# Norms between GEMMs in a two-layer encoder: one hand-ordered piece on TensorE, VectorE and ACT at each of four seams

## The chip, the cores and the metric

The kernel runs on one core of a Trainium2 chip. The metric is the device time of one execution in microseconds (us); a figure for a kernel is the median of its runs. TensorE (PE in the profile; PEld is its weight load) does the matmuls, VectorE (DVE) the elementwise arithmetic, ScalarE (ACT) the activation functions and casts, GpSimd (POOL) some elementwise work and the DMAs that it issues, SyncE (SP) most other DMAs. The kernel is written in a tile framework: a scheduler orders the instructions of every engine by priority (the order in which they are written) and by its own estimate of time, and places the semaphores. Inside `tc.manual_schedule(engines=...)` the named engines issue the region's instructions in the order in which they are written; where instructions from outside fall among them stays the scheduler's.

## The reference

Two layers over x of 1024 positions by 1024 channels, float32. Cut to what matters here:

```python
def rmsnorm(x, g):
    xf = x.astype(jnp.float32)
    y = xf * lax.rsqrt(jnp.mean(xf * xf, axis=-1, keepdims=True) + EPS)
    return (y * g.astype(jnp.float32)).astype(x.dtype)

def conv_ffn(h, w_up, conv_w, conv_b, w_down):
    gate, val = jnp.split(h @ w_up, 2, axis=-1)
    gate = dwconv3(gate, conv_w, conv_b)
    return (jax.nn.silu(gate) * val) @ w_down

    for i in range(DEPTH):
        ...
        h = rmsnorm(x, norm1_g[i]) * (1.0 + sc1) + sh1
        if m == 0:
            y = attention_mixer(h, ...)      # ends in o @ w_o
        elif m == 1:
            y = hyena_mixer(h, ...)          # starts with h @ w_in, ends in zc @ w_out
        x = x + g1 * y
        h = rmsnorm(x, norm2_g[i]) * (1.0 + sc2) + sh2
        x = x + g2 * conv_ffn(h, ffn_w_up[i], ffn_conv_w[i], ffn_conv_b[i], ffn_w_down[i])
    return rmsnorm(x, final_g)
```

So a GEMM's result is scaled and added to x, x is normed over its channels, and the next GEMM takes the normed h. This happens between w_o and w_up (layer 0), w_down and w_in (layer 0 to layer 1), w_out and w_up (layer 1), and between w_down and the output (layer 1). These are the four seams, in this order.

## The kernel before

x lies with channels on partitions: eight tiles (k or dt_, 0 to 7) of 128 channels by 1024 positions. Positions are taken in two halves of 512 (`HS`, hf). Every GEMM runs in three matmuls per product: each operand is split into a high part in fp32r and a low part (the rest), and high by high, high by low and low by high are added up in PSUM. A weight tile of 128 by 1024 is loaded raw by SP, cast to its high part by ACT (L169, 128x1024) and subtracted to its low part by DVE (L162), or the low part is read from DRAM by a DMA that POOL issues (L173). `wt` is a set of two weight buffers used in turn; `wraw` two raw buffers.

**A seam.** `tail_begin` gives half of the PSUM tiles of the GEMM to four small tiles: two for results ("yt"), two for the norm ("nrm"); results then take turns in two halves of big tiles and two "yt" (`pst_tail`). For each half hf, and each output tile dt_ in it: the GEMM's matmuls for 128 channels by 512 positions (24 matmuls in the first seam, 6 in the second, 12 in the third and fourth), then `res` (L857): DVE adds the scaled result to x (`scalar_tensor_tensor`, STT, L858), ACT squares it (L861), DVE adds the square to the running sum `ssq` (L863), except for the last tile of the half, whose square is kept apart. Then `rstd_half` (L223): for each of four blocks of 128 positions TensorE sums `ssq` over the partitions by a matmul with ones (L226), and the last square likewise on top (L227); each of these fp32 matmuls is two instructions. ACT takes the root (L229), DVE the reciprocal (L230), and four transposes on TensorE (L232) spread it over the partitions of the "nrm" tile. `norm_half` (L243) then makes h for each of the eight tiles (`modnorm`): DVE scales x (L236), ACT adds the shift and rounds to h's high part (L238), DVE subtracts for the low part (L239). In the fourth seam DVE makes the output tile (L1705) and SP writes it out.

**The GEMMs behind the seams.** w_up: `ffn` (L947) loads a gate and a value weight tile and calls `gemm_h` (L276); for the first pair (`first=True`) half 0 of both stands before half 1, 96 matmuls in all; the second pair, 96 more, loads its gate weights into another pool. Then `differences` prepares sums of x and h on DVE and ACT for the following stage. w_in: `w_in_stream` (L1224) takes tiles 0, 1 and 2 of w_in together: half 0 of tiles 0 and 1, half 0 of tile 2, then half 1 likewise; tile 2's weights go into a pool (`fpool`) that is opened in the memory that the FFN of layer 0 has freed. The filter stage that runs beside it (`F.run`) also begins its loads there.

**What orders the work at the seams.** The scheduler alone, on all engines: it may put half 1's matmuls before half 0's, delay an add, or run a weight split between norm operations. In the third seam x is not in SBUF: `x[k]` and the first half of the w_out product, `y0`, are read from DRAM and added by DVE (L1673), with two buffers for `y0`.

Of the kernel before, what the change touches and what calls it, by code (L numbers as in the profile page):

```python
# [7 lines left out]
F32 = mybir.dt.float32  # L8
# [107 lines left out]
def tile_kernel(ctx: ExitStack, tc: tile.TileContext, t: dict):  # L116
# [106 lines left out]
    def rstd_half(hf, sq, pool, yt):  # L223
        for j in range(4):
            c0 = 512 * hf + j * P
            mm(yt[:, j:j + 1], lhsT=ssq[:, c0:c0 + P], rhs=ones[:, 0:1], start=True, stop=False)  # L226
            mm(yt[:, j:j + 1], lhsT=sq[:, j * P:(j + 1) * P], rhs=ones[:, 0:1], start=False, stop=True)  # L227
# [15 lines left out]
    def norm_half(hf, x, l, which, hd, pool, rs, bufs=4):  # L243
        for k in range(KT):
# [31 lines left out]
    def gemm_h(prs, hd, n=KT, first=False, start=True, stop=True):  # L276
        if first:
            order = [(hf, k, p_, i) for hf in range(2) for k in range(n) for p_ in prs for i in range(3)]
        else:
            order = [(hf, k, p_, i) for p_ in prs for k in range(n) for i in range(3) for hf in range(2)]  # L280
        for hf, k, ((wh, wl), pp), i in order:
            ks = slice(k * P, (k + 1) * P)
            mm(pp[:, HS[hf]], lhsT=(wh, wh, wl)[i][:, ks], rhs=hd[hf][i % 2][k],  # L283
               start=k == 0 and i == 0, stop=k == n - 1 and i == 2)

# [571 lines left out]
    def res(yp, x_t, g, cs, first, sq, last=False):  # L857
# [4 lines left out]
        if not first and not last:  # L862
            V.tensor_tensor(ssq[:, cs], ssq[:, cs], sq, op=ADD)  # L863
# [974 lines left out]
```

## Time and profile before

| | |
|---|---|
| median of 3 runs | 3000.87 us (2999.51 to 3001.46) |
| profiled execution | 2999.89 us |
| its span, first to last instruction | 2998.1 us |
| mean granted TensorE clock | 0.979 |
| PE busy | 2834.4 us, 95% |
| DVE busy | 2289.6 us, 76% |
| ACT busy | 1228.0 us, 41% |

How to read it: the page's first part gives each engine's busy time; its fourth part the chain of work that ended last, as shares of the span. In a line of the timeline stand the start in us from the span's start, the duration, the engine, the line of the kernel, the operation, output<-input by tile names, shape, and in brackets how long the engine had been idle before it and what ended that. In a line of the chain stand start, duration, engine, output and line. A waits line gives who waited for whom, the total in us, how often, and the longest. A windows line gives a stretch, its length, busy time and instruction count of each engine, the mean granted clock of TensorE (1.00 is full speed, 0.50 half), the DMA engines' share and GB/s. Tile names: wo_y, d_ps and wout_y are the results of w_o, w_down and w_out; g_ps and v_ps those of w_up; u_ps of w_in; xr, xd, xs are x in the three stages; fh_h, fh_l, gh_h, gh_l are h's high and low parts; tt is scaled x.

### The profile page before, as it was taken

Reading aid. Unit: us, or ns where it says so; the run is one execution under the profiler, and the core shown is the slowest. Engines: PE = TensorE matmul, PEld = TensorE weight load, DVE = VectorE, ACT = ScalarE, POOL = GpSimd, SP = SyncE. Lnnn points to the kernel's source line nnn. Section 1 sums busy time; section 2 is a strip of 40 time slices with the busy share of each in tenths; the row PEclk is TensorE's granted clock in tenths of the full one; section 3 lists DMA queues with packets and bytes.
Section 4 is the critical chain, followed back from the end, with each engine's and each line's share of the span. In section 5 each row is a group of like instructions: output and inputs, shape, how many; then the busy total and the mean of one; then the engine's idle time right before and its main releaser. Section 6 shows DMA issues by size and latency. Waiting matters only on the chain.

```text
span 2998.1 us, 36517 instructions
## 1 busy us (share of the span) xinstructions
PE 2834.4 (95%) x13152; PEld 2309.0 (77%) x13152; DVE 2289.6 (76%) x3017; ACT 1228.0 (41%) x1998; POOL 536.2 (18%) x452
## 2 busy tenths in 40 slices
PE   5989999999899999999889999999988999999998
PEld 4867777777677787888677878887866888887887
DVE  7788989856997776997667886788976867667544
ACT  3558888833444333334332232323333433333211
POOL 0064465200322232001000000000000323320000
PEclk9999999999999999999989999999998999999999
DMA  6252222132776423975446664665656222223321
GB/s 230 76 170 57 57 64 64 43 129 71 263 235 229 151 84 115 296 249 170 141 158 205 200 217 156 205 204 190 205 183 223 78 85 84 85 77 129 131 84 57
DMA packets 222040, 438.44 MB, mean 146 GB/s; under 512 B 21826, under 2 KB 116834, under 8 KB 217380
## 3 DMA queue, kind: packets, MB, share of 16 engines
q1 hardware_dynamic: 190052, 406.75, 40.1%
q0 software_dynamic: 31808, 29.37, 4.3%
q8 instruction: 104, 1.70, 0.2%
q14 instruction: 76, 0.62, 0.1%
HBM read 307.05 MB, written 128.99 MB: 145 GB/s over the span
## 4 chain that ended last, share of the span: by engine, by line
PE 72%; DVE 13%; DMA 9%; issue 3%; ACT 2%; POOL 1%; SPq 0%; DVEq 0%; ACTq 0%; POOLq 0%
PE w_ps L919 19%; PE d_ps L181 16%; PE u_ps L1278 6%; PE pt_ps L732 3%; PE wo_y L181 3%; PE ab_ps L1414 2%; PE qkv_mm L181 2%; PE o_ps L750 2%; PE o_ps L751 2%; PE s_ps L708 2%; PE s_ps L709 2%; PE g_ps L283 2%; DMA wld<-wi_raw 1%; PE f_ps L462 1%; PE f_ps L463 1%
## 5 line engine op out<-in xcount | busy, mean ns | idle before, releaser
L162 DVE TENSOR_TENSOR w_lo<-u,w_hi 128x1024 fp32r<-128x1024 f32 x120 | 180.5, 1505 | 62.6 <-ACT w_hi L1006 62.6
L1006 ACT CAST w_hi<-u 128x1024 fp32r<-128x1024 f32 x120 | 125.9, 1050 | 209.7 <-PE w_ps L919 204.1
L162 DVE TENSOR_TENSOR pT_lo<-pt_ps,pT_hi 128x512 fp32r<-128x512 f32 x256 | 167.9, 682 | 47.6 <-ACT pT_hi L737 45.5
L181 PE MATMUL d_ps<-s_lo,wd_hi 128*128 128x512 f32 x608 | 195.2, 390 | 0.0
L181 PE MATMUL d_ps<-s_hi,wd_lo 128*128 128x512 f32 x608 | 193.9, 390 | 0.0
L181 PE MATMUL d_ps<-s_hi,wd_hi 128*128 128x512 f32 x608 | 193.7, 391 | 0.0
L919 PE MATMUL w_ps<-t_h,w_hi 128*128 128x512 f32 x480 | 191.2, 398 | 2.5 <-ACT w_hi L1006 1.3
L919 PE MATMUL w_ps<-t_l,w_hi 128*128 128x512 f32 x480 | 190.5, 397 | 0.0
L919 PE MATMUL w_ps<-t_h,w_lo 128*128 128x512 f32 x480 | 189.1, 395 | 0.6 <-DVE w_lo L162 0.6
L1112 DVE SCALAR_TENSOR_TENSOR xd<-d_ps,mod,xd 128x1024 f32<-128x1024 f32 x104 | 132.8, 1281 | 67.8 <-PE d_ps L181 67.5
L737 ACT CAST pT_hi<-pt_ps 128x512 fp32r<-128x512 f32 x256 | 144.9, 588 | 71.3 <-PE pt_ps L732 64.5
L716 DVE TENSOR_REDUCE nmx<-s_ps 128x1 f32<-128x1024 f32 x128 | 155.6, 1217 | 12.8 <-PE s_ps L709 10.8
L732 PE MATMUL pt_ps<-ident,p_t 128*128 128x128 f32 x1024 | 154.2, 274 | 10.3 <-DVE pT_lo L162 9.3
L732 PEld LDWEIGHTS pt_ps<-ident,p_t 128*128 128x128 f32 x1024 | 126.5, 141 | 45.3 <-DVE pT_lo L162 7.7
L919 PE MATMUL w_ps<-fh_h,w_hi 128*128 128x512 f32 x320 | 127.6, 399 | 19.5 <-ACT w_hi L1006 14.6
L726 ACT ACTIVATE p_t<-s_ps,nmx 128x1024 f32<-128x1024 f32 x128 | 143.7, 1124 | 3.1 <-DVE nmx L716 1.9
L1278 PE MATMUL u_ps<-fh_h,w_lo 128*128 128x512 f32 x384 | 140.3, 421 | 2.2 <-DMA w_lo<-wld 2.2
L1027 POOL TENSOR_TENSOR s<-u 128x512 f32<-128x512 f32 x40 | 53.9, 1347 | 487.6 <-DVE w_lo L162 221.5
L1278 PE MATMUL u_ps<-fh_l,w_hi 128*128 128x512 f32 x384 | 136.3, 418 | 1.8 <-DVE fh_l L239 1.8
L1278 PE MATMUL u_ps<-fh_h,w_hi 128*128 128x512 f32 x384 | 131.4, 416 | 3.4 <-ACT fh_h L238 3.4
L181 PEld LDWEIGHTS d_ps<-s_hi,wd_hi 128*128 128x128 f32 x608 | 113.7, 188 | 24.0 <-issue 0.9
L181 PEld LDWEIGHTS d_ps<-s_lo,wd_hi 128*128 128x128 f32 x608 | 113.7, 188 | 23.2 <-issue 0.4
(394 smaller groups left out, 7686.4 us busy)
## 6 DMA issues: line engine op xcount, KB each, us to landing
u<-in_w_up_dram SPq DMA_DIRECT2D x80, 512.0 KB
w_raw<-in_w_down_dram SPq DMA_DIRECT2D x44, 512.0 KB
sg<-gate SPq DMA_DIRECT2D x40, 512.0 KB
w_raw<-sg SPq DMA_DIRECT2D x40, 512.0 KB
w_raw<-in_ada_w_dram SPq DMA_DIRECT2D x32, 512.0 KB
m_raw<-in_ada_t_dram SPq DMA_DIRECT2D x32, 512.0 KB
ed<-eo SPq DMA_DIRECT2D x64, 256.0 KB
eo<-ed SPq DMA_DIRECT2D x16, 1024.0 KB
```

The costliest lines, as they stand in the source:

```text
L162: V.tensor_tensor(lo, src, hi.bitcast(F32), op=SUB)
L181: mm(out[:, cs], lhsT=a, rhs=b[:, cs], start=start and i == 0, stop=stop and i == 2)
L283: mm(pp[:, HS[hf]], lhsT=(wh, wh, wl)[i][:, ks], rhs=hd[hf][i % 2][k], start=k == 0 and i == 0, stop=k == n - 1 and i == 2)
L708: mm(s_ps[:, cs], lhsT=qg[u][:, i], rhs=kTh[g][:, cs], start=True, stop=False)
L716: V.tensor_reduce(nmx, s_t[u, i], op=ALU.max, axis=AX.X, negate=True)
L726: nc.scalar.activation(p_t, s_ps, AF.Exp, bias=nmx, accum_out=sums[u][:, i:i + 1])
L732: nc.tensor.transpose(tp[:, i * P:(i + 1) * P], pts[u, i][:, sb * P:(sb + 1) * P], ident)
L737: nc.scalar.copy(ph, pt_t[u, sb][0])
L919: mm(out, lhsT=(w[0], w[0], w[1])[i][:, k * P:(k + 1) * P], rhs=b[i % 2][k], start=k == 0 and i == 0, stop=k == 3 and i == 2)
L1006: nc.scalar.copy(w[0], src)
L1112: V.scalar_tensor_tensor(x[dt_], yp, gate[dt_], x[dt_], op0=MUL, op1=ADD)
L1278: mm(yp[:, HS[hf]], lhsT=(wh, wh, wl)[i][:, k * P:(k + 1) * P], rhs=hd[hf][i % 2][k], start=k == 0 and i == 0, stop=k == KT - 1 and i == 2)
```

## The change

A function `seam` now writes each seam as one region with a fixed order on TensorE, DVE and ACT.

- All tiles of half 0 come first, each with its result (`res`, now always with the add to `ssq`, but for the first tile of the second and fourth seams, whose square starts the sum).
- Then half 1's tiles. After 11 of their matmuls TensorE takes half 0's sums (`rstd_sums`; one matmul per block instead of two, with root and reciprocal behind), after 17 the transposes (`rstd_spread`). From then on `per` norm operations of half 0 follow each result of half 1 (6, 1, 3 and 2 in the four seams); what is left follows the last result.
- Then the next GEMM's first matmuls on half 0 run, and the two events of half 1 come after `at` matmuls of it: (12, 18), (26, 44), (20, 27); in the fourth seam at once. All norm operations of half 1 are written behind the transposes.
- The norm operations are written as scale 0, scale 1, low 0, scale 2, low 1, and so on (`norm_ops`), each scale with its ACT operation.
- In the first and third seams the next GEMM's first pair, both halves, lies in the region (`first_two`); in the second, half 0 of w_in tiles 0 and 1 (`w_in_half`). Their weights are loaded ahead: in the first seam after half 1's second tile, which frees the buffers (half 1 takes the tiles in the order 7, 5, 6); in the second and third seams ahead of the region. In `w_in_stream` half 1 of tiles 0 and 1 now follows half 0 of tile 2 as before, without their half 0.

The core of the diff (call sites that only pass the new arguments are left out; `step` and `result` of the second and third seams are like those of the first):

```diff
+    nsd = const.tile([P, 2, 4], F32, name="nsd")
+
+    def rstd_sums(hf, yt):
         for j in range(4):
             c0 = 512 * hf + j * P
-            mm(yt[:, j:j + 1], lhsT=ssq[:, c0:c0 + P], rhs=ones[:, 0:1], start=True, stop=False)
-            mm(yt[:, j:j + 1], lhsT=sq[:, j * P:(j + 1) * P], rhs=ones[:, 0:1], start=False, stop=True)
-        sd = pool.tile([P, 4], F32, name="nrm_sd", tag="nrm_sd", bufs=2)
-        nc.scalar.activation(sd, yt[:, 0:4], AF.Sqrt, bias=eps, scale=1.0 / D)
-        V.reciprocal(sd, sd)
+            mm(yt[:, j:j + 1], lhsT=ssq[:, c0:c0 + P], rhs=ones[:, 0:1], start=True, stop=True)
+        nc.scalar.activation(nsd[:, hf], yt[:, 0:4], AF.Sqrt, bias=eps, scale=1.0 / D)
+        V.reciprocal(nsd[:, hf], nsd[:, hf])
+
+    def rstd_spread(hf, yt):
         for j in range(4):
-            nc.tensor.transpose(yt[:, j * P:(j + 1) * P], sd[:, j:j + 1].to_broadcast([P, P]), ident)
-        return yt
+            nc.tensor.transpose(yt[:, j * P:(j + 1) * P], nsd[:, hf, j:j + 1].to_broadcast([P, P]), ident)
+
+    def seam(n, step, result, ops, tps, at, per, nxt=()):
+        todo = []
+
+        def run(k):
+            for _ in range(min(k, len(todo))):
+                todo.pop(0)()
+
+        def events(hf, a, b):
+            yt = nrm_tile(tps)
+
+            def spread():
+                rstd_spread(hf, yt)
+                todo.extend(ops(hf, yt))
+            return [(a, lambda: rstd_sums(hf, yt)), (b, spread)]
+
+        def fire(ev, m):
+            while ev and m >= ev[0][0]:
+                ev.pop(0)[1]()
+
+        with tc.manual_schedule(engines={mybir.EngineType.PE, mybir.EngineType.DVE, mybir.EngineType.Activation}):
+            for i in range(n):
+                for _ in step(0, i):
+                    pass
+                result(0, i)
+            ev, m = events(0, 11, 17), 0
+            for i in range(n):
+                for _ in step(1, i):
+                    m += 1
+                    fire(ev, m)
+                result(1, i)
+                if not ev:
+                    run(per)
+            run(len(todo))
+            ev, m = events(1, *at), 0
+            for _ in nxt:
+                m += 1
+                fire(ev, m)
+                run(len(todo))
+            fire(ev, at[1])
+            run(len(todo))
...
+    def norm_ops(hf, x, l, which, hd, pool, rs, bufs=4):
+        b = [mod[:, l, 3 * which, k:k + 1] for k in range(KT)]
+        tt = {}
+
+        def scale(k):
             x_k = x[k][:, HS[hf]]
-            tt = x_k if pool is None else pool.tile([P, 512], F32, name="tt", tag="tt", bufs=bufs)
-            modnorm(x_k, k, l, which, rs, hd[hf][0][k], hd[hf][1][k], tt)
+            tt[k] = x_k if pool is None else pool.tile([P, 512], F32, name="tt", tag="tt", bufs=bufs)
+            V.scalar_tensor_tensor(tt[k], x_k, acol[:, l, which, k:k + 1], rs, op0=MUL, op1=MUL)
+            nc.scalar.activation(hd[hf][0][k], tt[k], AF.Identity, bias=b[k])
+
+        def low(k):
+            V.scalar_tensor_tensor(hd[hf][1][k], tt[k], b[k], hd[hf][0][k].bitcast(F32), op0=ADD, op1=SUB)
+        order = [(scale, 0)] + [p_ for k in range(1, KT) for p_ in ((scale, k), (low, k - 1))] + [(low, KT - 1)]
+        return [lambda f=f, k=k: f(k) for f, k in order]
...
-        if not first and not last:
+        if not first:
             V.tensor_tensor(ssq[:, cs], ssq[:, cs], sq, op=ADD)
...
+    ORD = ((5, 6, 7), (7, 5, 6))
+    yps, pre = {}, []
+
+    def wo_step(hf, i):
+        yps[hf, i] = pst_tail(tps, "wo_y")
+        w, cs = wl3[ORD[hf][i] - 5], HS[hf]
+        for k in range(KT):
+            ks = slice(k * P, (k + 1) * P)
+            for j, (a, b) in enumerate(((w[0], oh), (w[0], ol_), (w[1], oh))):
+                mm(yps[hf, i], lhsT=a[:, ks], rhs=b[k][:, cs], start=k + j == 0, stop=k == KT - 1 and j == 2)
+                yield
+
+    def wo_res(hf, i):
+        dt_ = ORD[hf][i]
+        res(yps[hf, i], x[dt_], mod[:, 0, 2, dt_:dt_ + 1], HS[hf], False, sq_tile(sp_))
+        nc.sync.dma_start(xsd[0][dt_][:, HS[hf]], x[dt_][:, HS[hf]])
+        if hf and i == 1:
+            pre.extend(load_split(t["w_up"][0, 0, j], wt.pools[j], 1) for j in range(2))
+
+    def first_two(l, pre):
+        pre += [pst("g_ps"), pst("v_ps")]
+        yield from gemm_h([(pre[0], pre[2]), (pre[1], pre[3])], hd, True)
+
+    seam(3, wo_step, wo_res, lambda hf, yt: norm_ops(hf, x, 0, 1, hd, None, yt), tps, (12, 18), 6, first_two(0, pre))
...
+    def w_in_half():
+        ws = [wt.load(t["w_in"][ct], wld[ct]) for ct in range(2)]
+
+        def go():
+            w_in2.extend((w, pst("u_ps")) for w in ws)
+            yield from gemm_h(w_in2, hd, True, range(1))
+        return go()
...
+    pre = [wt.load(t["w_up"][1, 0, i]) for i in range(2)]
...
+    seam(KT - 2, wout_step, wout_res, lambda hf, yt: norm_ops(hf, x, 1, 1, hd, None, yt), tps, (20, 27), 3,
+         first_two(1, pre))
```

More of the change, by code (lines that the diff above doesn't have):

```diff
@@ L911, in tile_kernel @@
     wt.pools.pop().release()
-    wt.i = 0
+    wt.i = 2
     ot_pool.release()
@@ L945, in tile_kernel, with ffn @@
     hn = ("fh", "gh")
-    def ffn(l, base, work, tail, more=None):
+    def ffn(l, base, work, pre, ops, per, at, nxt, more=None):
         nonlocal x, hd, h_pools
@@ L985, in ffn @@
         for f in range(NPL[l]):
-            if f == 1:
+            if f == 0:
+                gp, vp = pre[2:]
+            else:
                 gw = load_split(t["w_up"][l, f, 0], None, None, dst=[u_tile(F32R) for _ in range(2)])
-            else:
-                gw = wt.load(t["w_up"][l, f, 0])
-            vw = wt.load(t["w_up"][l, f, 1])
-            gp, vp = pst("g_ps"), pst("v_ps")
-            gemm_h([(gw, gp), (vw, vp)], hd, first=f == 0)
+                vw = wt.load(t["w_up"][l, f, 1])
+                gp, vp = pst("g_ps"), pst("v_ps")
+                for _ in gemm_h([(gw, gp), (vw, vp)], hd):
+                    pass
             times(f, gated(f, gp), vp)
@@ L1137, in ffn, with step, result @@
             pass
-        for hf in range(2):
-            for dt_ in range(KT):
-                yp = pst_tail(tps, "d_ps")
-                down(yp, dt_, HS[hf], grp)
-                sq = tp_.tile([P, 512], F32, name="sq", tag="tt", bufs=4)
-                res(yp, x[dt_], gate[dt_], HS[hf], dt_ == 0, sq, dt_ == KT - 1)
-            tail(hf, tp_, rstd_half(hf, sq, tp_, nrm_tile(tps)))
+        yps = {}
+        def step(hf, dt_):
+            yps[hf, dt_] = pst_tail(tps, "d_ps")
+            ds, cs = slice(dt_ * P, (dt_ + 1) * P), HS[hf]
+            for i, (sh, sl, wh, wl) in enumerate(grp):
+                for j, (a, b) in enumerate(((wh, sh), (wh, sl), (wl, sh))):
+                    mm(yps[hf, dt_], lhsT=a[:, ds], rhs=b[:, cs], start=i + j == 0, stop=i == len(grp) - 1 and j == 2)
+                    yield
+        def result(hf, dt_):
+            res(yps[hf, dt_], x[dt_], gate[dt_], HS[hf], dt_ == 0, tp_.tile([P, 512], F32, name="sq", tag="tt", bufs=4))
+        seam(KT, step, result, lambda hf, yt: ops(hf, tp_, yt), tps, at, per, nxt() if nxt else ())
         tail_end(tps, False)
@@ L1258, in w_in_stream @@
             if ct < 3:
-                first.append(((wh, wl), pst("u_ps") if ct < 2 else y1.tile([P, L], F32, name="u_ps", tag="y")))
-                if ct < 2:
-                    continue
-                order = [(hf, k, c_, i) for hf in range(2) for cs in ((0, 1), (2,)) for k in range(KT)
+                first.append(((wh, wl), y1.tile([P, L], F32, name="u_ps", tag="y")))
+                order = [(hf, k, c_, i) for hf, cs in ((0, (2,)), (1, (0, 1)), (1, (2,))) for k in range(KT)
                          for c_ in cs for i in range(3)]
@@ L1700, in tile_kernel, with ops1, out @@
     z_pool.release()
-    def tail1(hf, pool, rs):
-        for k in range(KT):
+    def ops1(hf, pool, rs):
+        def out(k):
             o_t = pool.tile([P, 512], F32, name="o_t", tag="o_t", bufs=4)
@@ L1706, in tail1 @@
             nc.sync.dma_start(t["out"][k][:, HS[hf]], o_t)
-    ffn(1, "right", "left", tail1)
+        return [lambda k=k: out(k) for k in range(KT)]
+    ffn(1, "right", "left", pre, ops1, 2, (0, 0), None)
     wt.release()
```

63 lines of the change are left out of this document (30 added, 33 removed).

## The prediction

> **What bounds the kernel now.** I read the page first (busy shares, then the chain that ended last), then the busy time by windows around the four norms, then the waits, the chain and the timeline inside each. The page says that TensorE is the bound:
>
> ```profile
> span 2998.1 us, 36517 instructions
> PE 2834.4 (95%) x13152; PEld 2309.0 (77%) x13152; DVE 2289.6 (76%) x3017; ACT 1228.0 (41%) x1998; POOL 536.2 (18%) x452
> PE 72%; DVE 13%; DMA 9%; issue 3%; ACT 2%; POOL 1%; SPq 0%; DVEq 0%; ACTq 0%; POOLq 0%
> ```
>
> A change at the norms can win only what TensorE loses there. The windows view, cut at the four seams (columns: stretch, its length, busy us and instructions of PE, PEld, DVE, ACT, POOL, mean granted clock, DMA share, GB/s):
>
> ```profile
> 673.40:764.00 90.60, 85.05 (x377) 68.70 (x375) 64.55 (x94) 38.48 (x55) 0.00 (x0) 0.96 0.25 88
> 1477.70:1543.60 65.90, 57.78 (x234) 45.62 (x234) 46.88 (x72) 29.63 (x42) 1.59 (x3) 0.86 0.47 166
> 2256.40:2352.60 96.20, 88.04 (x380) 71.85 (x379) 77.74 (x109) 39.93 (x59) 2.34 (x2) 0.91 0.45 160
> 2938.40:2994.90 56.50, 48.78 (x232) 40.58 (x230) 32.07 (x47) 11.81 (x19) 0.00 (x0) 0.93 0.17 64
> ```
>
> Full-clock prices come from the chain. 48 matmuls in a row take 10.88, so 0.227 each. Sixteen sum instructions (the first and last of eight pairs stand here) run from 1498.31 to 1499.99, 0.105 each:
>
> ```profile
> 1498.31 0.12 PE nrm L226 x2
> ...
> 1499.77 0.22 PE nrm L227 x2
> ...
> 2341.82 10.88 PE v_ps L283 x48
> ```
>
> First seam (w_o to w_up): 144 tail and 192 w_up matmuls are 76.2, 32 sum instructions 3.4 and the transposes about 0.9, together 80.5 of 90.6: 10 us are lost, to waits and to a halved clock behind them. The waits view has the longest; the windows show the clock:
>
> ```profile
> PE g_ps L283 <- DVE xr L236: 3.2, 1, 3.2
> ```
>
> ```profile
> 724.40:727.80 3.40, 0.72 (x2) 0.30 (x2) 3.40 (x6) 3.40 (x6) 0.00 (x0) 1.00 0.00 0
> 727.80:734.60 6.80, 6.06 (x14) 4.31 (x15) 6.80 (x12) 3.53 (x6) 0.00 (x0) 0.50 0.01 2
> 1540.10:1543.60 3.50, 1.33 (x6) 0.75 (x5) 3.40 (x4) 3.25 (x3) 1.05 (x2) 0.99 1.05 417
> 1543.60:1547.00 3.40, 3.33 (x8) 2.66 (x9) 3.40 (x7) 1.04 (x1) 0.00 (x0) 0.50 1.05 417
> ```
>
> Behind 2.7 us of idling come 6.8 us in which 14 matmuls run where 30 fit; behind 2.2 us come 3.4 us at half. So a stall of 2 us or more costs its length and 1.7 to 3 us of clock.
>
> **The change's price on VectorE.** Now DVE and ACT obey the written order. A result is a scalar_tensor_tensor (STT, L858), ACT's square, then the add (L863), and the next STT stands behind that add. In the first seam the old kernel happens to run so; the timeline of DVE and ACT shows the unit costs:
>
> ```profile
> 673.30 1.06 ACT L169 CAST w_hi<-w_raw 128x1024 fp32r<-128x1024 f32 x1 [2.07 <-PE wo_y L181]
> 674.86 1.22 DVE L162 TENSOR_TENSOR w_lo<-w_raw,w_hi 128x1024 fp32r<-128x1024 f32 x1
> 678.97 0.75 DVE L858 SCALAR_TENSOR_TENSOR xr<-wo_y,mod,xr 128x512 f32<-128x512 f32 x1 [1.70 <-PE wo_y L181]
> 680.48 0.69 DVE L863 TENSOR_TENSOR ssq<-ssq,sq 128x512 f32<-128x512 f32 x1 [0.76 <-ACT sq L861]
> 703.49 5.36 DVE L236 SCALAR_TENSOR_TENSOR xr<-xr,acol,nrm 128x512 f32<-128x512 f32 x8
> ```
>
> From STT to add is 1.51, the add 0.6 more before DVE goes on: 2.1 us for each result, 0.84 of it over what the two operations occupy. A norm operation takes 5.36/8 = 0.67.
>
> **First seam.** Half the sum instructions go: 16 by 0.105 = 1.7 saved. A tile's 24 matmuls take 5.44. Counted from the end of half 1's first tile, DVE does a result and six norm operations (6.1), then a result, two weight splits of 1.22 and six more (8.6): at 14.7 it takes up the last tile, finished at 10.9. That tile's add ends at 16.9; TensorE, 12 matmuls past 10.9, wants the sums at 13.6 and waits 3.3, with handovers up to 4. The reciprocal, behind four norm operations, adds 0.8. Stalls 4.5 and half clock 2.7 (as after the old 3.2 us stall) replace 10: with the sums 4.5 gained. DVE is busy without a break behind the norm and still owes the split (1.22) of the second w_up tile's weights: I take **-3.3**, bounds -7 (no stall) and 0 (DVE sets the next stage's start).
>
> **Second seam (w_down to w_in).** A tile is six matmuls, 1.36 us, against 2.1 on DVE. The old order never paid the wait: four STTs come first, and half 1's adds come behind half 0's norm. The timeline of DVE (one row of ACT), then the chain:
>
> ```profile
> 1478.64 2.36 DVE L162 TENSOR_TENSOR wd_lo<-w_raw,wd_hi 128x1024 fp32r<-128x1024 f32 x2 [0.39 <-ACT wd_hi L169]
> 1483.48 1.05 ACT L169 CAST w_hi<-w_raw 128x1024 fp32r<-128x1024 f32 x1 [4.88 <-DMA w_raw<-in_w_in_dram]
> 1484.86 2.73 DVE L858 SCALAR_TENSOR_TENSOR xd<-d_ps,mod,xd 128x512 f32<-128x512 f32 x4 [3.86 <-PE d_ps L181]
> 1515.51 4.67 DVE L863 TENSOR_TENSOR ssq<-ssq,sq 128x512 f32<-128x512 f32 x6
> 1531.99 2.74 DVE L239 SCALAR_TENSOR_TENSOR fh_l<-tt,mod,fh_h 128x512 fp32r<-128x512 f32 x4
> ```
>
> ```profile
> 1533.32 1.42 DVE fh_l L239 x2
> ...
> 1535.33 8.30 DMA w_lo<-wld
> 1543.62 0.04 issue
> 1543.67 12.28 PE u_ps L1278 x46
> ```
>
> The last low part (1534.74) frees the memory into which the third w_in tile is loaded, and 8.9 us later its matmuls begin, whatever TensorE did meanwhile. So the seam is priced by when DVE ends. Before: 1484.86 to 1534.74, 49.9. After, from the first STT: half 0 takes 0.7 plus 0.7 until the next tile plus seven results, 16.1; sums, root and reciprocal 3.1, with half 1's first STT inside; seven results 14.7; sixteen norm operations 10.7; about 2.6 until the 44th matmul lets the transposes pass; sixteen more operations and one handover 11.2: 58.4. It starts earlier: tile 0 needs the second wd_lo, there at 1481.0, so the first STT is at 1481.5 where it was at 1484.86. It ends at 1539.9, 5.2 later. Behind it in the ordered queues wait PSUM tiles, so TensorE idles some 4 us before half 0's sums and 9 us in pieces at the first w_in tiles, which need low parts. That halves the clock, as above; six matmuls then take 2.5 where DVE makes a tile in 1.33, so the 44th comes about 2 later. A half-clock window behind the longer wait for the third tile's weights adds up to 1.7. I take **+8**, bounds +5 and +10.
>
> [...]
>
> **Third seam (w_out to w_up).** Half 0 of all tiles now comes before half 1, and each tile's x is completed by L1673 from two loads. The chain, and the timeline of DVE:
>
> ```profile
> 2253.40 12.88 DMA w_raw<-in_w_up_dram
> ...
> 2271.70 21.11 PE wout_y L181 x80
> ```
>
> ```profile
> 2268.53 2.35 DVE L1673 TENSOR_TENSOR xs<-xs,y 128x1024 f32<-128x1024 f32 x2
> 2275.54 1.23 DVE L1673 TENSOR_TENSOR xs<-xs,y 128x1024 f32<-128x1024 f32 x1 [0.41 <-DMA y<-yd]
> 2277.53 1.22 DVE L1673 TENSOR_TENSOR xs<-xs,y 128x1024 f32<-128x1024 f32 x1
> 2283.53 1.22 DVE L1673 TENSOR_TENSOR xs<-xs,y 128x1024 f32<-128x1024 f32 x1
> 2285.45 1.22 DVE L1673 TENSOR_TENSOR xs<-xs,y 128x1024 f32<-128x1024 f32 x1
> ```
>
> The old order ran both halves of the early tiles while the last x came. In the new one half 0's sums stand 11 matmuls into half 1, need tile 7 and so come at about 2287.6 (the last L1673 perhaps a microsecond sooner, then STT, square, add); TensorE gets there at 2280 and waits 7 us. From there: sums 0.85, 61 tail matmuls 13.8, and 96 of w_up 21.8, with 2.2 for v_ps's PSUM tile, 1.2 for sums and reciprocal behind DVE (a result and three norm operations take 4.1 against a tile's 2.72), transposes 0.9, half clock 3; then 96 more, 21.8: 2353.2, with the two lots of w_up matmuls at 0.227, against 2352.6. With the SP queue now holding both w_up loads earlier, I take **+1**, bounds -6 (x arrives 8 sooner) and +6 (one such load more ahead of x).
>
> **Fourth seam.** In half 1 a result and two outputs take 3.44 against 2.72, so the last STT is 1.6 late; then come the add (0.69) and half the sums (0.85 less, and 0.85 less in half 0). **+0.5**, bounds 0 and +1.5.
>
> The rest I cost at nothing: nsd in constant memory replaces a pool tile; the w_in loads that move ahead of the tail are cast beside it already (1483.48); PSUM turns are renumbered. If that cover fails, a 1.06 cast and a 1.22 split are exposed.
>
> Sum: -3.3 + 8 + 1 + 0.5 = +6.2. The profiled execution took 2999.89 (span 2998.1), 0.98 under the median 3000.87; the median becomes **3007**.
>
> **The rivals.** About 6 us (0.2%) is what a measurement here can tell from no change.
> (a) *The squares do not hold DVE up*: another operation stands in each wait, or the adds slip one result. Place: DVE in every seam; price: the 0.84 per add, 11.8 in the second seam. It decides once more than half of the 0.84 is filled. The second seam then ends 5 early, the first wins 5, the third 3, the fourth 1: 2987. For it: the old trace's six adds in a row; against it: the order is now literal. Chance 0.23.
> (b) *The third w_in tile's load is released earlier than by the last low part* (its neighbour in time is the scale operation's last read of x). Then only TensorE's own end, about 2 late, counts in the second seam: 3001. Against it: the load left 0.6 us behind the last low part. 0.19.
> [...] 0.12.
> (d) *x comes later still in the third seam*: +6 there, 3012. 0.09.
> (e) My forecast, 0.37.
>
> **How the numbers follow.** Faster by over 0.2% is (a): 0.23. Within it are (b) and (c) and a little of (e): 0.33. Slower is most of (e) and (d): 0.44. The range runs from (a)'s 2987, with 3 for the spread of its four terms, to 3016, where the upper bounds of the second and third seams meet half way; (e) alone has 3000 to 3014, so both signs hold much of the chance.
>
> **What would show it.** In the new profile: on DVE in the second seam pairs of STT and add 1.5 apart with 0.76 of waiting on ACT's square; the last low part some 7 us later against the first w_down tail matmul; a gap of 6 us or more on TensorE before the third w_in tile; sums of half 0 in the third seam waiting on tile 7; in the first seam one stall of 3 to 4 us at half 1's sums. I am wrong if the second seam's DVE chain is under 52 us, or if TensorE's clock stays at 1.00 there.

## The result, and the profile after

| | before | after |
|---|---|---|
| median | 3001.16 us, 4 runs (2999.51 to 3003.79) | 3023.85 us, 4 runs (3022.09 to 3029.34) |
| profiled span | 2998.1 us | 3021.4 us |

The changed kernel is slower: ratio 1.0078, 95% interval 1.006 to 1.0095, so 18 to 28 us, 22.7 by the medians. I had +6.2.

The page of the changed kernel: span, busy time by engine, and the share of the engines in the chain that ended last.

```profile
span 3021.4 us, 36385 instructions
PE 2835.5 (94%) x13088; PEld 2303.7 (76%) x13088; DVE 2299.9 (76%) x3025; ACT 1230.9 (41%) x1998; POOL 537.6 (18%) x452
PE 66%; DVE 17%; DMA 9%; ACT 4%; issue 3%; SPq 0%; DVEq 0%; ACTq 0%; POOLq 0%
```

TensorE is busy for 1.1 us more than before (2834.4), with 64 sum instructions fewer; its idle time grew by 22 of the 23 us. VectorE's share of the chain went from 13 to 17%. The windows view, cut at the four seams at the same places of the work as the rows of before:

```profile
677.20:765.10 87.90, 83.16 (x361) 67.32 (x359) 66.71 (x97) 39.27 (x55) 2.39 (x2) 0.96 0.27 95
1480.40:1553.60 73.20, 57.91 (x218) 43.99 (x218) 49.03 (x74) 30.34 (x42) 1.59 (x3) 0.85 0.41 141
2275.30:2377.30 102.00, 85.59 (x366) 67.24 (x365) 79.84 (x111) 42.00 (x60) 1.18 (x1) 0.97 0.42 157
2961.00:3018.20 57.20, 47.12 (x216) 38.56 (x215) 33.40 (x49) 11.92 (x19) 0.00 (x0) 0.94 0.16 63
```

Against 90.60, 65.90, 96.20 and 56.50 us: -2.7, +7.3, +5.8 and +0.7. That is 11 of the 23 us; the other 12 came up between the seams.

**First seam.** TensorE's timeline (first row: idle time and releaser in brackets) and the windows behind it:

```profile
718.48 1.86 PE L228 MATMUL nrm<-ones,ssq 128*128 128x1 f32 x8 [3.83 <-DVE ssq L916]
```

```profile
715.10:718.50 3.40, 0.02 (x1) 0.02 (x1) 3.40 (x6) 2.30 (x4) 0.00 (x0) 0.82 0.95 322
718.50:721.90 3.40, 3.40 (x12) 3.11 (x13) 2.75 (x5) 0.87 (x2) 0.00 (x0) 0.50 0.69 245
```

One stall of 3.83 us at half 1's sums, and a clock of 0.50 in the 3.40 us behind it.

**Second seam.** VectorE's timeline, then the chain:

```profile
1490.47 0.74 DVE L911 SCALAR_TENSOR_TENSOR xd<-d_ps,mod,xd 128x512 f32<-128x512 f32 x1
1491.91 0.69 DVE L916 TENSOR_TENSOR ssq<-ssq,sq 128x512 f32<-128x512 f32 x1 [0.70 <-ACT sq L914]
1492.52 0.74 DVE L911 SCALAR_TENSOR_TENSOR xd<-d_ps,mod,xd 128x512 f32<-128x512 f32 x1
```

```profile
1488.24 1.05 ACT w_hi L169
1489.29 0.54 ACT sq L914
1489.86 0.69 DVE ssq L916
...
1545.49 0.76 DVE fh_l L296
1546.84 6.74 DMA w_lo<-wld
1553.62 9.94 PE u_ps L1364 x35
```

STT, square, add, STT, 2.05 us for each result; the first square stands behind a cast on ACT; the third w_in tile's load leaves 0.6 us behind the last low part.

**Third seam.** TensorE's timeline, each row the first matmul behind a wait, then VectorE's:

```profile
2306.75 1.87 PE L228 MATMUL nrm<-ones,ssq 128*128 128x1 f32 x8 [7.49 <-DVE ssq L916]
...
2326.84 0.50 PE L335 MATMUL v_ps<-gh_h,w_hi 128*128 128x512 f32 x1 [1.77 <-DVE xs L911]
2332.66 1.05 PE L228 MATMUL nrm<-ones,ssq 128*128 128x1 f32 x8 [1.63 <-DVE ssq L916]
2335.61 0.65 PE L234 MATMUL nrm<-ident,nsd 128*128 128x128 f32 x4 [0.18 <-DVE nsd L230]
2346.00 0.50 PE L335 MATMUL g_ps<-gh_l,w_hi 128*128 128x512 f32 x1 [0.27 <-DVE gh_l L296]
2348.59 0.50 PE L335 MATMUL g_ps<-gh_l,w_hi 128*128 128x512 f32 x1 [0.91 <-DVE gh_l L296]
2351.17 0.50 PE L335 MATMUL g_ps<-gh_l,w_hi 128*128 128x512 f32 x1 [0.94 <-DVE gh_l L296]
```

```profile
2337.62 1.29 DVE L997 TENSOR_TENSOR xs<-xs 128x512 f32<-128x512 f32 x2
2338.83 0.74 DVE L296 SCALAR_TENSOR_TENSOR gh_l<-xs,mod,gh_h 128x512 fp32r<-128x512 f32 x1
...
2341.47 1.29 DVE L162 TENSOR_TENSOR t_l<-xs,t_h 128x512 fp32r<-128x512 f32 x2
```

The stall of 7.49 us is followed by 5.7 us of waits in six pieces. The last three are low parts: VectorE's operations of `differences` (L997, and L162 for t_l), which are not of the region, fall between the region's, and the low parts come behind them.

**Between the seams.** Ahead of the first seam, between the second and third, and behind the third every engine issues the same instructions in the same order in both kernels, but for a handful; between the first and second some 80 of VectorE's 670 instructions and 46 of TensorE's 3056 stand in another place. Still the changed kernel loses 3.8 us ahead of the first seam, 1.6 between the first and second, 8.8 behind the second up to the third, and wins 2.1 behind the third: 12.0, and with the seams' 11.3 (by the stretches below) the span's 23.3. The 2.1 belong to the trace of before: all but one of the other traces here, that with every seam old among them, are shorter there by 2.1 to 2.2. One place of the 8.8, behind the second seam: SP issues a load of `eo`, VectorE waits for it, TensorE for VectorE. SP's and VectorE's timelines of before, then SP's, VectorE's and TensorE's of the changed kernel:

```profile
1692.79 0.32 SPq L441 DMA_DIRECT2D eo<-ed  x1
```

```profile
1700.36 0.41 DVE L446 TENSOR_TENSOR eo<-eo,srow 1x256 f32<-1x256 f32 x1 [1.27 <-DMA eo<-ed]
```

```profile
1703.38 0.32 SPq L494 DMA_DIRECT2D eo<-ed  x1
```

```profile
1712.93 0.41 DVE L499 TENSOR_TENSOR eo<-eo,srow 1x256 f32<-1x256 f32 x1 [3.02 <-DMA eo<-ed]
```

```profile
1717.15 0.94 PE L515 MATMUL f_ps<-ri,dftf 128*128 128x256 f32 x2 [2.17 <-DVE ri L352]
```

The same load is used 7.6 us behind its issue before, 9.6 after; the 2 us become a stall of 2.17, where it was 0.41, and with a clock of 0.56 in the 3.40 us from 1717.00 TensorE falls back by 3.4 us more. A place ahead of the first seam, worth 2.5 of the 3.8, stands in the last section.

### The profile page after: what moved, and what is told of

Read it like the earlier page. It is cut to its first block, busy times and chain, and to the rows that moved or that the text cites. A ratio compares the mean times of both kernels' runs of the same rounds, so it can differ in the third digit from the quotient of the medians.

```text
span 3021.4 us, 36385 instructions
## 1 busy us (share of the span) xinstructions
PE 2835.5 (94%) x13088; PEld 2303.7 (76%) x13088; DVE 2299.9 (76%) x3025; ACT 1230.9 (41%) x1998; POOL 537.6 (18%) x452
## 4 chain that ended last, share of the span: by engine, by line
PE 66%; DVE 17%; DMA 9%; ACT 4%; issue 3%; SPq 0%; DVEq 0%; ACTq 0%; POOLq 0%
PE w_ps L987 20%; PE d_ps L181 14%; PE u_ps L1364 4%; PE pt_ps L785 3%; PE ab_ps L1500 2%; PE qkv_mm L181 2%; PE wo_y L181 2%; PE o_ps L803 2%; PE o_ps L804 2%; PE s_ps L761 2%; PE s_ps L762 2%; PE f_ps L181 1%; PE f_ps L515 1%; DMA wld<-wi_raw 1%; PE f_ps L516 1%
## 5 line engine op out<-in xcount | busy, mean ns | idle before, releaser
L162 DVE TENSOR_TENSOR w_lo<-u,w_hi 128x1024 fp32r<-128x1024 f32 x120 | 180.1, 1501 | 62.4 <-ACT w_hi L1075 62.4
L162 DVE TENSOR_TENSOR pT_lo<-pt_ps,pT_hi 128x512 fp32r<-128x512 f32 x256 | 167.8, 681 | 46.4 <-ACT pT_hi L790 44.5
L181 PE MATMUL d_ps<-s_lo,wd_hi 128*128 128x512 f32 x544 | 170.1, 390 | 0.0
L181 PE MATMUL d_ps<-s_hi,wd_lo 128*128 128x512 f32 x544 | 168.5, 390 | 0.0
L181 PE MATMUL d_ps<-s_hi,wd_hi 128*128 128x512 f32 x544 | 168.5, 390 | 0.0
L987 PE MATMUL w_ps<-fh_h,w_hi 128*128 128x512 f32 x320 | 128.4, 401 | 21.0 <-ACT w_hi L1075 13.3
L1364 PE MATMUL u_ps<-fh_h,w_lo 128*128 128x512 f32 x368 | 132.0, 417 | 4.9 <-DMA w_lo<-wld 4.9
L1500 PE MATMUL ab_ps<-prod,dfti 128*128 128x256 f32 x512 | 124.0, 386 | 9.9 <-ACT abx L1504 3.1
L987 PE MATMUL w_ps<-fh_h,w_lo 128*128 128x512 f32 x320 | 127.0, 398 | 2.6 <-DVE w_lo L162 2.6
L1364 PE MATMUL u_ps<-fh_l,w_hi 128*128 128x512 f32 x368 | 128.2, 414 | 0.1
L987 PE MATMUL w_ps<-fh_l,w_hi 128*128 128x512 f32 x320 | 127.1, 397 | 0.0
```

The source lines that it names most:

```text
L162: V.tensor_tensor(lo, src, hi.bitcast(F32), op=SUB)
L181: mm(out[:, cs], lhsT=a, rhs=b[:, cs], start=start and i == 0, stop=stop and i == 2)
L987: mm(out, lhsT=(w[0], w[0], w[1])[i][:, k * P:(k + 1) * P], rhs=b[i % 2][k], start=k == 0 and i == 0, stop=k == 3 and i == 2)
L1364: mm(yp[:, HS[hf]], lhsT=(wh, wh, wl)[i][:, k * P:(k + 1) * P], rhs=hd[hf][i % 2][k], start=k == 0 and i == 0, stop=k == KT - 1 and i == 2)
L1500: mm(ap[:, i], lhsT=dfti[:, m, :], rhs=v, start=n == 0, stop=n == len(ops) - 1)
```

## The experiments

The edits are shown cut down to what they change; switches are left out. A reading of one trace by stretches goes with each run. First: from the tail's first w_o matmul to the first matmul behind the second w_up pair (91.4 us before). Second: from the tail's first w_down matmul to the 301st of w_in (134.6). Third: from the 192nd w_out matmul to the first behind the second w_up pair (119.0). Fourth: from the tail's first w_down matmul to the end (59.9). The changed kernel's four against before's: -2.7, +7.5, +5.9, +0.6. How far they can be trusted: in kernels that leave a seam as before, its stretch reads +0.3 to +0.5, -3.6 to -0.1, -2.5 to +0.1, and -0.5 to +0.4. So the one trace of before reads its own seams long, by 2.5 us in all: against the mean of the kernels with the seam old (before's 0 among them: +0.3, -1.6, -1.0, -0.3) the changed kernel's four are -3.0, +9.0, +6.8 and +0.9, together 13.8. The ratios are to the kernel before on the same chip.

**One seam alone.** The loops of before are put back beside the new ones; four kernels have one `1` each.

```diff
+    NEWS = (1, 0, 0, 0)
...
+    if NEWS[0]:
         seam(3, wo_step, wo_res, ...)
+    else:
+        for hf in range(2):
+            ...
```

> The first seam alone in the new form, the other three in the old one. In the trace of the changed kernel the same matmuls move by -2.7 us against before between the start of the first tail and the end of its second w_up pair. Theory A (each seam costs what its own stretch shows, and the rest of the +22.7 us is timing that does not belong to this seam): -2.7 us, 2998.5. Theory B (the 3.8 us that the changed kernel loses ahead of the first seam come with the new constant tile, so with every kernel that has it): +1.1 us.

Measured: 2998.46 against 2998.67 us, ratio 1.0004 (0.9993 to 1.0015); its stretch -3.9.

> The second seam alone in the new form. Its own stretch shows +7.4 us in the trace of the changed kernel; behind it, in the filter stage and the stage after, another 8.8 us come up. Theory A (only the stretch itself is its cost): +7.4 us, 3008.6. Theory B (what follows in the filter stage is its consequence, the 3.8 ahead of the first seam come with the constant tile): +16 to +20 us.

Measured: 3011.51, ratio 1.0042 (1.0027 to 1.0056); stretch +7.4.

> The third seam alone in the new form. Its own stretch shows +5.9 us, where I had +1. Theory A: +5.9 us, 3007. Theory B (3.8 more with the constant tile): +9.7 us. Theory C (the stretch was late only because it was entered at another phase of the x loads): +1 us as forecast.

Measured: 3010.39, ratio 1.004 (1.0026 to 1.0055); stretch +7.0.

> The fourth seam alone in the new form. Its stretch shows +1.2 us. Theory A: +1.2 us, 3002.4. Theory B (3.8 more with the constant tile): +5 us. Until the last tail this kernel issues the same instructions in the same order on every engine as the one before, with one small constant tile more in memory, so its trace also shows whether the 3.8 us ahead of the first seam are there without any seam.

Measured: 3002.95, ratio 1.0014 (1.0002 to 1.0026); stretch +1.5.

The stretches repeat those of the changed kernel, so each is its seam's own. The second and third carry the loss. The medians lie 3 to 5 us above the stretches, which is neither of A nor plainly B; B's cause, the constant tile, is tested next.

**The constant tile.** The old loops four times, with `nsd` allocated and unused; and the reverse, the change with `nsd` in a pool of the tail.

```diff
-    NEWS = (1, 1, 1, 1)
+    NEWS = (0, 0, 0, 0)
```

> All four seams in the old form; the only difference from the kernel before is the small constant tile nsd, which nothing uses. Every engine issues the same instructions in the same order as before. The four single seams came out 3 to 5 us above what their own stretches show (-3.7, +7.7, +6.9, +1.5 in their traces against medians of -0.2, +12.8, +11.7, +4.3). Theory A (the rest is the spread of executions): 0 us, the same time as before. Theory B (the constant tile moves the other tiles in memory and costs time everywhere): +4 us.

Measured: 2998.82, ratio 1.0001 (0.9991 to 1.001).

```diff
-        nc.scalar.activation(nsd[:, hf], yt[:, 0:4], AF.Sqrt, bias=eps, scale=1.0 / D)
+        sds[hf] = sdp[0].tile([P, 4], F32, name="nrm_sd", tag="nrm_sd", bufs=2)
+        nc.scalar.activation(sds[hf], yt[:, 0:4], AF.Sqrt, bias=eps, scale=1.0 / D)
```

> The changed kernel with nsd in the pools of the tails, as before, instead of in constant memory. Theory A (nsd's place is without effect): 3023, as the changed kernel. Theory B (the constant tile costs 4 us everywhere): 3019.

Measured: 3021.65, ratio 1.008 (1.0067 to 1.0093); stretches -3.4, +8.3, +6.7, +1.6. The tile's place does nothing. In the trace of the unused tile the stage ahead of the first seam is 2.3 us longer than before, with the same instructions; over all the kernels here that stage reads -4.1 to +5.3. So the 3.8 lie within what this stage does by itself. The stage between the second and third seams, +8.8 in the changed kernel, is +2.1 in the run with `nsd` in a pool, which issues the same order there; but that trace is of an execution 6.9 us under its kernel's median, so whether the 8.8 come with the change stays open.

**The adds.**

```diff
     def res(yp, x_t, g, cs, first, sq):
         V.scalar_tensor_tensor(x_t[:, cs], yp, g, x_t[:, cs], op0=MUL, op1=ADD)
+        add_owed()
         nc.scalar.activation(sq, x_t[:, cs], AF.Square)
-            V.tensor_tensor(ssq[:, cs], ssq[:, cs], sq, op=ADD)
+            owed_add.append(lambda: V.tensor_tensor(ssq[:, cs], ssq[:, cs], sq, op=ADD))
```

> The changed kernel with each add to ssq written behind the next result's STT, so that VectorE no longer stands waiting for ACT's square (0.76 us at each add in the trace). Theory A (this wait is the second seam's cost, as my forecast said): the second seam's stretch goes from +7.4 us to about -4, the first and third gain 2 us each, in all 12 to 16 us less than the changed kernel, about 3010. Theory B (TensorE's stalls and its half clock set the seam's end, VectorE follows): within 4 us of the changed kernel.

As it ran, this kernel leaves out the adds of the seams' results altogether, so ssq lacks those squares: it shows what the seams cost without the adds and the wait. Measured: 2986.91, ratio 0.9958 (0.9943 to 0.9973); stretches -4.5, -7.1, +0.2, -3.2.

> The changed kernel with each add to ssq in the seams written behind the next result's STT (the run before this one that was meant to do so left the adds of the seams out). All adds are there. Theory A (VectorE's wait for the square, 0.76 us at each add, sets the second seam's end, as my forecast said): second seam's stretch from +7.4 to about -3, first and third 2 us less each, fourth 1 less: 15 us under the changed kernel, about 3007. Theory B (it is not the wait but the add itself, 0.6 us of VectorE, that counted when the adds were left out): within 5 us of the changed kernel's 3022.

Measured: 3006.59, ratio 1.003 (1.0018 to 1.0042); stretches +0.1, -2.7, +7.1, -0.2. VectorE's timeline in the second seam, and the chain:

```profile
1491.17 0.74 DVE L949 SCALAR_TENSOR_TENSOR xd<-d_ps,mod,xd 128x512 f32<-128x512 f32 x1
1491.83 0.68 DVE L956 TENSOR_TENSOR ssq<-ssq,sq 128x512 f32<-128x512 f32 x1
```

```profile
1535.45 7.74 DMA w_lo<-wld
1543.24 10.67 PE u_ps L1440 x35
```

The add now follows the STT by 0.66 instead of 1.44, with nothing waited for; the third w_in tile's matmuls start at 1543.24. The second seam is settled: 10 us of wait for the square. The first and third don't follow, so theory A's time of 3007 was met in part by luck: the median fell by 15 us, the four stretches together by 7. In the first and third the last add of half 1 had come to stand behind the norm operations that follow the last result, so:

```diff
                 result(1, i)
+                if i == n - 1:
+                    add_owed()
                 if not ev:
                     run(per)
```

> As the run with each add behind the next STT, in all four seams, but the last add of half 1 stands directly behind its STT and square, ahead of the norm operations. Theory A (the last add behind the norm operations hid the gain in the first and third seams): first stretch from +0.1 to -4, third from +7.2 to +4, time 3000 where that run took 3006.6. Theory B (the third seam loses to the order of its halves, not to adds): first -4, third still +6 to +7, time 3003.

Measured: 3008.71, ratio 1.0038 (1.0024 to 1.0053); stretches -2.8, -3.0, +4.3, -0.4. The first is back at the change's own value, the third 1.6 us under it, the median no better and 6 to 9 us above the two theories. Most of what the wait costs lies in the second seam. (Without any adds the third read +0.2: there the adds themselves cost, not only the wait.)

**The order of the halves in the third seam.**

```diff
-            for i in range(n):
-                for _ in step(0, i):
+            head = [(hf, i) for i in range(early) for hf in range(2)] + [(0, i) for i in range(early, n)]
+            for hf, i in head:
+                for _ in step(hf, i):
                     pass
-                result(0, i)
+                result(hf, i)
             ev, m = events(0, 11, 17), 0
-            for i in range(n):
+            for i in range(early, n):
```

> The third seam alone in the new form, but both halves of its first four tiles come before half 0 of the last two, so that only 24 of half 1's matmuls follow half 0's sums and TensorE has work until the last x is there. Theory A (the stall of 7.5 us ahead of half 0's sums is what the seam costs): the stall shrinks to 1 or 2 us, 9 us less than before in the stretch, against +6.9 with the third seam as in the change: about 2990 where the third seam alone gave +11.7. Theory B (the low parts behind it, delayed by other VectorE work, set the end): still within 3 us of the third seam alone.

Measured: 3007.22, ratio 1.0035 (1.0022 to 1.0047); stretch +4.1, about theory B's 3 us under the third seam alone. TensorE's timeline:

```profile
2299.93 1.05 PE L258 MATMUL nrm<-ones,ssq 128*128 128x1 f32 x8 [2.28 <-DVE ssq L958]
2310.53 0.80 PE L373 MATMUL g_ps<-gh_h,w_hi 128*128 128x512 f32 x1 [4.41 <-ACT gh_h L331]
```

The stall of 7.5 is 2.28, as A has it, and comes back a little later as 4.41: too little of half 1 is left to cover half 0's norm, and VectorE still takes 2.1 to 3.5 us for each of ten results in a row (2276.09 to 2299.87).

> As the run with each add behind the next STT, and in the third seam both halves of its first four tiles come before half 0 of the last two. Theory A (the third seam loses to half 0's sums waiting for the last x, and once the tiles are turned to VectorE, which takes 2.1 us for each result): third seam's stretch 6 to 8 us less than in the run with the adds alone, about 3000. Theory B (too few of half 1's matmuls are left to cover half 0's norm, 4.4 us of stall in the run with the tiles turned): within 3 us of the run with the adds alone.

Measured: 2998.37, ratio 0.9997 (0.9987 to 1.0008); stretches +0.1, -3.9, -1.3, -0.8. Both together end the third seam's loss: 8.4 us less in its stretch than with late adds alone.

```diff
-    NEWS, DEFER = (1, 1, 1, 1), (1, 1, 1, 1)
+    NEWS, DEFER = (1, 1, 0, 1), (1, 1, 0, 1)
```

> First, second and fourth seam new with each add behind the next STT, the third seam in the old form. Theory A (the rest of the loss is the third seam): 9 to 12 us under the run with the adds alone, at or a little under the kernel before, 2993 to 2998. Theory B (single seams don't add up): as the run with the adds alone.

Measured: 2999.1, ratio 1.0 (0.9991 to 1.001); the third stretch, old again, -1.8. Leaving the third seam out is worth the same as mending it.

**Only TensorE's order fixed.**

```diff
-        with tc.manual_schedule(engines={mybir.EngineType.PE, mybir.EngineType.DVE, mybir.EngineType.Activation}):
+        with tc.manual_schedule(engines={mybir.EngineType.PE}):
```

> The changed kernel with only TensorE's order fixed in the seams; VectorE and ACT are ordered by the scheduler, which by itself puts the adds of the second seam behind the next STT. Theory A (the literal order on VectorE is what costs): as the run with each add behind the next STT, about 3007. Theory B (the order on TensorE costs): as the changed kernel, 3022.

Measured: 2998.32, ratio 0.9998 (0.9988 to 1.0008); stretches -7.5, -2.3, +1.0, -0.2. The order on TensorE costs nothing; the order on VectorE and ACT together costs all of it, more than theory A had (which of the two engines, no run separates). Each against before on its chip, this median and the changed kernel's lie 23.3 us apart, and the four stretches show 20.3 of them: 4.8, 9.8, 4.8 and 0.8.

> Only TensorE's order is fixed in all four seams, and in the third both halves of the first four tiles come first. Theory A (the third seam's loss is the order of its halves, whoever orders VectorE): 2 to 6 us under the run with TensorE's order alone, 2992 to 2996. Theory B (the fixed VectorE order was the third seam's loss): the same 2998 as the run with TensorE's order alone.

Measured: 2997.41, ratio 0.9987 (0.9977 to 0.9997); third stretch +0.3: with VectorE free, turning the tiles is worth 0.8 us in its stretch, as theory B has it. The medians, -0.6 and -3.3 against before on their chips, are too near to tell A from B.

> The first seam alone in the new form, with only TensorE's order fixed. Theory A (VectorE's fixed order is what held the first seam back): stretch -7, time 2992 where the first seam alone with all three fixed gave the time of before. Theory B: as that run, 2998.

Measured: 2990.14 against 3000.69, ratio 0.996 (0.9948 to 0.9972); stretch -7.5. Its TensorE timeline at half 1's sums, and the windows there:

```profile
710.64 0.50 PE L373 MATMUL v_ps<-fh_h,w_lo 128*128 128x512 f32 x1 [1.09 <-DVE w_lo L162]
713.91 1.05 PE L258 MATMUL nrm<-ones,ssq 128*128 128x1 f32 x8 [1.39 <-DVE ssq L958]
```

```profile
708.80:712.20 3.40, 2.31 (x11) 1.51 (x9) 3.40 (x6) 1.85 (x3) 0.00 (x0) 1.00 0.97 252
712.20:715.60 3.40, 2.01 (x13) 1.57 (x12) 1.73 (x4) 0.26 (x1) 0.00 (x0) 1.00 0.98 355
```

Two stalls of 1.09 and 1.39 us replace the one of 3.83, and the clock stays at 1.00. This is the fastest complete kernel here, 2 us under theory A.

> All four seams new: the first with only TensorE's order fixed, the second to fourth with each add behind the next STT, the third with both halves of its first four tiles first. Theory A (the fixed order on VectorE costs the first seam 5 to 7 us, and seams add up): 7 us under the run with late adds and turned tiles, about 2991. Theory B (seams do not add up; later stages wait for something else): the same 2998.

Measured: 2992.98, ratio 0.9972 (0.9961 to 0.9983); stretches -7.5, -4.1, -1.3, -1.0.

> First seam with only TensorE's order fixed, second and fourth with each add behind the next STT, third in the old form. Theory A (seams add up): stretches of -7.5, -4 and -1, about 2988 to 2991. Theory B: 2998 as the run with the third seam old and all adds late.

Measured: 2993.02, ratio 0.9972 (0.9961 to 0.9984); stretches -7.5, -3.7, -0.1 (old), -0.2. Neither is under the first seam alone: the new second to fourth seams, mended, add nothing to it.

**Why VectorE's freedom helps the first seam.** VectorE's timeline of the changed kernel, then of the first seam alone with only TensorE fixed. In the one it stands idle from the reciprocal to the next result; in the other it takes up the norm there, behind the transposes:

```profile
697.60 0.18 DVE L230 RECIPROCAL nsd<-nsd 128x4 f32<-128x4 f32 x1 [1.45 <-ACT nsd L229]
700.89 0.75 DVE L911 SCALAR_TENSOR_TENSOR xr<-wo_y,mod,xr 128x512 f32<-128x512 f32 x1 [3.11 <-PE wo_y L962]
```

```profile
694.10 0.18 DVE L261 RECIPROCAL nsd<-nsd 128x4 f32<-128x4 f32 x1 [1.45 <-ACT nsd L260]
695.74 4.70 DVE L330 SCALAR_TENSOR_TENSOR xr<-xr,acol,nrm 128x512 f32<-128x512 f32 x7 [1.46 <-PE nrm L265]
```

```diff
                 todo.extend(ops(hf, yt))
+                if n == 3 and hf == 0:
+                    run(4)
```

> The first seam alone in the new form, all three engines fixed as in the change, the adds as in the change, but four norm operations of half 0 stand directly behind the transposes and not behind the next result. Theory A (VectorE stands idle 3.1 us behind the reciprocal because its norm operations are written behind the next result, and that comes back as TensorE's stall at half 1's sums and its half clock): stretch from -3.9 to -7, the stall from 3.8 to about 1.5 us, time about 2992. Theory B (freedom of VectorE and ACT elsewhere is what helps): stretch stays at -3 to -4, time 2998.

Measured: 3002.64 against 2999.85, ratio 1.0009 (1.0 to 1.0017); stretch -0.5, and in TensorE's timeline the stall is longer:

```profile
712.73 1.87 PE L259 MATMUL nrm<-ones,ssq 128*128 128x1 f32 x8 [5.40 <-DVE ssq L963]
```

Theory A falls, and B missed too. Started early, all sixteen norm operations stand ahead of the last result, where four stood behind it; so the idle time filled is given back. In the run with VectorE free all sixteen stand ahead too, but no add waits for its square (three waits of 0.76). An early norm and late adds together, in a written order, were not run: that the two make the difference is argued from rows, not shown.

## Why the prediction was wrong

The first, second and fourth seams came out near their terms. Two steps failed: the third seam's sum, and the time outside the seams, which the sum put at nothing.

**The second seam: right in its mechanism, and in its size partly by luck.** +8 forecast, +7.5, +7.4 and +8.3 in three traces, by the mechanism given: pairs of STT and add 1.44 to 1.51 apart, the last low part releasing the load, half clock (0.85 over the seam, against 0.86 in a stretch 7 us shorter). Rival (a) falls: the order ran as written, with the waits in it, and writing the adds late removes them; (b) falls by the chain, in both kernels. Inside it two sizes were off, with opposite signs: VectorE's chain took 61.5 us (1484.70 to 1546.24), not 58.4 (or 60.4 with the 2 for the late 44th matmul), with 1.1 of it from the cast ahead of the first square, which the forecast had taken to be covered; and from the last low part to the third tile's matmuls it took 7.4, not 8.9, so TensorE's gap there was 4.89 (`u_ps <- DMA w_lo`), under the 6 that I named. The pieces at the first w_in tiles came to 5.2 us, not 9.

**The first: right in its stretch.** -3.3 forecast, -2.7, -3.4 and -3.9; one stall of 3.83 at half 1's sums against 3.3 "with handovers up to 4". Alone it doesn't show in the median.

**The fourth: right.** +0.5 forecast, +0.6 to +1.6 in three traces.

**The third: its sum failed behind the stall.** Half 0's sums came at 2306.75, 2287.85 on the clock of before (18.9 us of shift), where I had 2287.6, and the stall was 7.49 for 7. "From there" I had 65.6 us to the end of the second w_up pair; it took 70.5. The waits in the w_up part were 5.7, not the 3.4 of "2.2 for v_ps's PSUM tile, 1.2 for sums": low parts behind VectorE's operations from outside the region, 2.1 of the 5.7, had no place in the sum. The rest of the 4.9 is half 1's sums (1.05), for which the sum had no term, and 192 w_up matmuls that took 45.6 us, not 43.6; half clock (0.50 in the 3.40 us from 2306.70, 0.82 in the next) cost 2.5, not 3. The seam ended at +5.9, at the bound of +6 that I had given. The wider loss, that half 0's sums need the last x and stand in front of work that doesn't, I had seen and taken to be paid back; turned tiles with late adds show 8.4 us in it.

**The total: the step that failed is "the rest I cost at nothing".** The sum -3.3 + 8 + 1 + 0.5 has the four seams in it and no term for the stages between them, and no reason why they should keep their times. In the changed kernel's trace these stages have 12.0 of the 23.3 us. The four stretches sum to 11.3 there and to 13.3 in the other trace of the same order, 13.8 and 15.7 against the mean of the kernels with old seams; the medians say 22.7 and 24.0. Against the medians my sum lacks 16 us: 5 in my four terms by the trace of before, nearly all of them in the third, and the rest outside the stretches. The constant tile is not the cause. Stages with the same order spread by 9 us between kernels, so what one trace shows there can't be put down to the change. Nor do the medians tie it to the number of new seams: they lie above the sum of the stretches by 3.3 to 11.4 us in kernels with several new seams (the late adds: 4.4 against 7.7; only TensorE fixed: -9.0 against -0.6), and by 0.4 to 8.9 in those with one or none (2.3 with none; -10.9 against -10.6 for the first seam alone with VectorE free). The stage behind the second seam reads +4.8 on average where the second seam is new and +2.2 where it is old, single values -0.8 to +8.8. Two places were followed, the load of `eo` and VectorE's operations beside POOL's; what moves these stages as a whole stays open. My range held only the seams. Its top of 3016 doesn't come out of their bounds either: with the second and third at their upper bounds the sum is 3014, with all four 3018, and the measured 3023.85 is above both.

The clock's price, "a stall of 2 us or more costs its length and 1.7 to 3 us of clock", doesn't hold in general: the last section shows a stall of 2.75 us with the clock at 1.00 ahead of it and behind it.

## What to carry to other kernels

Fix the order of the engine that sets the end, and leave the others to the scheduler until a trace shows that they need it: here the same TensorE order cost nothing with VectorE and ACT free and 23 us with all three written out. 10 of these are VectorE's waits for ACT's square in the second seam. If an engine's order is written, put what consumes another engine's result one step late. Putting matmuls that are ready ahead of those that wait for late data won 8.4 us in the third seam, with late adds; doing the like with VectorE's norm operations lost 3 us in the first, so an idle gap that a trace shows is not yet a gain. Before a difference of a few us in one stage is explained, look at how the same stage reads in kernels that don't change it.

## What the runs showed of the hardware

**The clock.** Stalls of 1.09 and 1.39 us in neighbouring stretches left the granted clock at 1.00 (the first seam alone with only TensorE's order fixed); one of 2.17, that of the `eo` load in the changed kernel, was followed by a clock of 0.56 (windows of the changed kernel):

```profile
1713.60:1717.00 3.40, 1.38 (x7) 0.84 (x5) 3.37 (x6) 0.81 (x2) 0.00 (x0) 1.00 0.36 120
1717.00:1720.40 3.40, 3.25 (x9) 2.66 (x9) 3.40 (x8) 0.00 (x0) 0.00 (x0) 0.56 0.10 34
```

In these traces neither the length of a stall nor the busy time around it settles this. In the same kernel TensorE waited 2.75 us, busy for 1.48 us of the 3.40 from 1652.60 (1.38 in the first row above), and the clock stayed at 1.00 (timeline, then the window around the end of the stall):

```profile
1656.83 0.63 PE L1316 MATMUL u_tr<-ident,u 128*128 128x128 f32 x4 [2.75 <-DVE u L342]
```

```profile
1656.00:1659.40 3.40, 2.57 (x16) 2.24 (x17) 2.49 (x4) 1.09 (x2) 0.00 (x0) 1.00 0.80 292
```

And in the kernel before, 2.29 us of busy time in 3.40 (2297.90 to 2301.30, mostly sum instructions and transposes) were followed by a clock of 0.50 to 2311.50. In the first seam two short stalls (1.09 and 1.39 us) in place of one of 3.83 saved the half clock as well (1.00 against 0.50); that this would happen elsewhere is not shown.

**VectorE beside POOL.** Ahead of the first seam, VectorE's and POOL's timelines of the changed kernel, then the same matmul on TensorE in the changed kernel and in the one before:

```profile
173.25 0.69 DVE L658 TENSOR_TENSOR qk_a<-qk_a,qk_b 128x512 f32<-128x512 f32 x1
...
177.24 2.93 DVE L653 TENSOR_TENSOR qk_a<-qk_n,Tq 128x512 f32<-128x512 f32 x1
180.20 2.73 DVE L658 TENSOR_TENSOR qk_a<-qk_a,qk_b 128x512 f32<-128x512 f32 x1
```

```profile
171.48 5.75 POOL L189 TENSOR_SCALAR w_raw<-w_raw,csil 128x1024 f32<-128x1024 f32 x2 [7.36 <-DMA w_raw<-in_ada_w_dram]
177.21 5.17 POOL L190 TENSOR_TENSOR ssq<-ssq,w_raw 128x1024 f32<-128x1024 f32 x2
```

```profile
183.58 0.51 PE L181 MATMUL qkv_mm<-w_hi,hh 128*128 128x512 f32 x1 [2.98 <-DVE qk_n L652]
```

```profile
181.16 0.50 PE L181 MATMUL qkv_mm<-w_hi,hh 128*128 128x512 f32 x1 [0.50 <-DVE qk_n L599]
```

An operation that takes 0.69 us beside POOL's `tensor_scalar` (first row of each timeline) takes 2.73, and the one ahead of it 2.93, while POOL runs two `tensor_tensor` of 2.6. TensorE then waits 2.98. In the kernel before, with the same order on every engine here, one such operation was held up ahead of this matmul and not two (2.77 us from 177.73, beside a pair of POOL's `tensor_tensor` that began at 176.99), and TensorE waited 0.50: this place alone sets the two traces 2.5 us apart, of the 3.8 ahead of the first seam. The long operations here fall together with POOL's `tensor_tensor`; the one at 177.02 in the kernel before, where that pair begins, still took 0.68. Which operations meet would hang on when POOL's loads land (7.36 us of waiting for one, in the row above); that is argued, not shown, and how much of the other differences between stages of the same order comes from it stays open.
